# Post-norm chains on the vector engine by pairs of k-tiles, and 1/rms of memory attention in the exponential

## The chip, the cores and the metric

One core of one Trainium2 chip runs the whole program. The metric is the device time of one execution in microseconds (us). Engines: TensorE (PE, with its weight loads as PEld), the vector engine (DVE), the scalar engine (ACT), GpSimd (POOL), and the queue that issues most DMAs (SP). Each runs its own instruction queue in order; they wait for one another through semaphores.

## The reference

Two transformer blocks in float32 on 512 tokens of width 1024. The change lies in the second block, between its mixer and its feed-forward layer:

```python
def rms_norm(x, g):
    y = x * lax.rsqrt(jnp.mean(x * x, axis=-1, keepdims=True) + RMS_EPS)
    return y * g

# second_block
x = x + rms_norm(merged @ w_mix_out, mix_post_g)
h = rms_norm(x, xa_pre_g)
x = x + rms_norm(mem_attention(h, mem_n, w_xq, w_xkv, w_xo), xa_post_g)
h = rms_norm(x, ffn_pre_g)
x = x + rms_norm(conv_ffn(h, w_up, conv_w, conv_b, w_down), ffn_post_g)

# mem_attention: 4 heads of 128, 256 memory tokens
q = h @ w_xq;  s = q @ k.T / sqrt(128);  p = softmax(s);  o = p @ v;  return o @ w_xo
```

## The kernel before

Activations lie with features on the 128 partitions and the 512 tokens along the free axis, so a tensor of width 1024 is 8 k-tiles of 128 x 512. `X` is the running sum x. Every matmul in float32 precision is three matmuls in a reduced form (lines L195 to L197, in `mm3`): operands are split into a rounded part (`qhi`, `whi`) and its residue (`qlo`, `wlo`). Weights are loaded tile by tile and split by `wsplit`: the cast on the scalar engine (L186), the subtraction (L187) on the vector engine, or on GpSimd if the caller says so (`lo_eng`).

The work around the change runs over two halves of the tokens, 256 columns each (`HALVES`). `fm` computes output tiles m one after the other, and between the matmuls it takes steps of a generator (`between`), which holds the chain of the half before. The order in which the queues hold the work comes from a scheduler that follows the program's order and priorities, not from a table.

The stages, with their tiles: the merge projection (`w_mix_out`, 8 tiles, the last 5 in halves); the query projection of memory attention (`w_xq`, 4 tiles, one for each head) and its output projection (`w_xo`, 8 tiles of 4 k-tiles), both for the first half and then for the second; the first three pairs of tiles of the up projection (`w_up`), in halves, then the others over 512 columns.

`post` makes what stands between two projections. `ev` evicts a tile times its gain into `Y` (`Ym` or `KV`), and adds its square to `sqs`. `after` is the chain of a half: 1/rms of the tile (`r_post`, by sums over partitions in TensorE and `rms`), its broadcast over partitions (`bcast`, L330, copied to `rbp`), and then for each of the 8 k-tiles Y times `rbp` (L1404), X plus Y (L1405), the split of X times the next gain into `qhi` and `qlo` (`pre`, L1357 and L1358), and the square of X (L1411), of which GpSimd adds up two groups of four (L1415). These are summed by TensorE (`sums`, L312) into `r_pre`, the 1/rms of the next norm, which is broadcast into `rb`. The next projection runs on X times gain, and its result is multiplied by `rb` when it leaves the accumulator: L1643 for the query (`xq`), L1723 for the up projection (`z`).

`head_half` is one head for one half: `xq`; for each 128 tokens the scores (L1647), their maximum (L1652), the exponential with its sum (L1654), reciprocal and normalisation; then transposes (L1668), the product with v (L1673), and the split of the result into `xh` (L1674, L1675), which the output projection reads. `pair2` evicts a pair of tiles of the up projection, applies the convolution and the Gelu (L1733).

Of the kernel before, what the change touches and what calls it, by code (L numbers as in the profile page):

```python
# [10 lines left out]
F32 = mybir.dt.float32  # L11
# [9 lines left out]
S = 512  # L21
# [38 lines left out]
LQ, LO = 0, 1  # L60
# [20 lines left out]
def kernel(ctx: ExitStack, tc: tile.TileContext, a: dict, out: bass.AP, stop=None):  # L81
# [43 lines left out]
    def col(name, i):  # L125
        o = COLS[name][0] + i
        return cols[:, o:o + 1]
# [1054 lines left out]
    X = []  # L1182

    def load_x():
        for i, tag in enumerate(("og", "cg")):
            t = xs.tile([128, 4, S], F32, tag=tag, name=f"X{i}")
            nc.sync.dma_start(t, a["xT"][:, 4 * i:4 * i + 4])
            X.extend(t[:, k] for k in range(4))

# [73 lines left out]
    def add_sq(src, m, x, y, eng=V):  # L1263
        if m == 0:
            A.activation(sqs[:, x:y], src, AF.Square)
        else:
            t = sp.tile([128, S], F32, tag="sqt", name="sqt")
            A.activation(t[:, x:y], src, AF.Square)
            eng.tensor_tensor(sqs[:, x:y], sqs[:, x:y], t[:, x:y], ALU.add)
# [115 lines left out]
    def post(Y, gname, nextg, g2):  # L1385

        def ev(m, x, y, p):
            if YA and y - x < S:
                A.activation(Y(m, x, y), p, AF.Copy, scale=col(gname, m))
            else:  # L1390
                V.tensor_scalar(Y(m, x, y), p, col(gname, m), None, ALU.mult)
            add_sq(p, m, x, y, G if AQ and y - x < S else V)

        def after(x, y):
            rbp = sp.tile([128, S // 2], F32, tag="rbp", name="rbp")
            r = fm_stats(sp, sqs[:, x:y], "post")
            yield
            bcast(rbp, r)
            pt = sums()
            for k in range(KT + PL):  # L1400
                if k > 1:
                    yield
                if k < KT:
                    V.tensor_tensor(Y(k, x, y), Y(k, x, y), rbp, ALU.mult)  # L1404
                    (V if k in XV else G).tensor_tensor(X[k][:, x:y], X[k][:, x:y], Y(k, x, y), ALU.add)  # L1405
                j = k - PL
                if j >= 0:
                    pre(g2, nextg, j, x, y)
                    first, end = j in SQS, j + 1 in SQS
                    t = sp.tile([128, S // 2], F32, tag="n2t" if first else "sqx", name="sqx")  # L1410
                    A.activation(t, X[j][:, x:y], AF.Square)  # L1411
                    if first:
                        held = t
                    else:
                        G.tensor_tensor(held, held, t, ALU.add)  # L1415
                    if end and j < KT - 1:
                        tc.cur_priority += SL
                        sum_sq(pt, held, j + 1 == SQS[1], False)
                        tc.cur_priority -= SL
            yield  # L1420
            sum_sq(pt, held, len(SQS) == 1, True)
            r = rms(sp, pt, (y - x) // 128, "pre")
            yield
            bcast(rb[:, x:y], r)
        return ev, after

# [195 lines left out]

    xa = ExitStack()
# [6 lines left out]
    ev, after = post(lambda k, x, y: Ym[:, k, x:y], "mix_post_g", "xa_pre_g", g4)  # L1630
# [9 lines left out]
    def head_half(h, x, y, p):  # L1640

        xq = xt.tile([128, S // 2], F32, tag="xq", name="xq")
        V.tensor_tensor(xq, p, rb[:, x:y], ALU.mult)  # L1643
        soft = []
        for t in range((y - x) // 128):
# [5 lines left out]
            sc = 128 ** -0.5  # L1651
            V.tensor_reduce(mx, s_[:, :MEM], AX, ALU.max)  # L1652
            V.tensor_scalar(mx, mx, -sc, None, ALU.mult)
# [36 lines left out]
    ev, after = post(lambda k, x, y: KV[:, k] if x else Ym[:, k, x:y], "xa_post_g", "ffn_pre_g", g4)  # L1690
# [20 lines left out]
    with tc.tile_pool(name="fp2", bufs=1) as fp:  # L1711
        zl = fp.tile([128, 2, 4, 2], F32, name="zl")

        def pair2(pg_, pu_, i, x, y, held):
            res = []
# [189 lines left out]
```

## Time and profile before

| | |
|---|---|
| Timed runs (3) | 1681.08, 1681.2, 1683.91 us; median 1681.2 |
| Profiled execution | 1677.47 us, span of its instructions 1675.7 us |
| Mean granted clock of TensorE | 0.984 |
| Busy: TensorE, vector, scalar, GpSimd | 96%, 57%, 43%, 19% |

A busy share is an average over all stages. What a stage can gain is read from the windows and waits of that stage. A time in the timeline is counted from the start of the span; the matmuls' ends are modelled, so that the distance of two starts says more than a duration. "Granted clock" is the share of TensorE's full rate of 2.4 GHz; half of it is 1.2 GHz.

### The profile page before, as it was taken

To read this page: it belongs to the slowest core of one execution; us is meant where nothing else is said; L and a number is where in the kernel's file an instruction comes from. 1 tells how busy PE (TensorE), PEld (TensorE's weight loads), DVE (VectorE), ACT (ScalarE), POOL (GpSimd) and SP (SyncE) were. 2 spreads that over 40 slices of the span, in tenths; PEclk is the share of its full clock that TensorE was granted. 3 is DMA by queue.
4 is the path that set the end of the run, shared out by engine and by line. 5 is a ranking of instruction groups with operands and counts; after the bars stand their busy time and mean duration, and the time that the engine had idled before them with its cause. 6 is when DMAs were issued, how large, how long until landed. Compare 5 with 4: busy or idle time off the path is not lost.

```text
span 1675.7 us, 25585 instructions
## 1 busy us (share of the span) xinstructions
PE 1605.1 (96%) x10116; PEld 1362.9 (81%) x10116; DVE 954.5 (57%) x1728; ACT 721.6 (43%) x1374; POOL 325.5 (19%) x354
## 2 busy tenths in 40 slices
PE   9999989989999999999999999999888999999997
PEld 6898777668899888888888777888887888888886
DVE  6547887777666222223335776345677877776233
ACT  4525455566645322232223664234455544444221
POOL 1313310231111222210004000132423222221002
PEclk9999999989999999999999999999899899999998
DMA  9222244231323333333332212335110233233332
GB/s 377 60 80 65 95 142 156 68 122 64 126 76 102 91 98 99 91 97 102 88 115 85 63 39 64 101 95 181 42 35 26 76 101 97 92 101 94 95 92 73
DMA packets 47465, 161.95 MB, mean 97 GB/s; under 512 B 5488, under 2 KB 10096, under 8 KB 45552
## 3 DMA queue, kind: packets, MB, share of 16 engines
q1 hardware_dynamic: 44752, 157.74, 29.7%
q10 hardware_dynamic: 2304, 2.29, 0.4%
q8 instruction: 80, 1.31, 0.3%
q0 software_dynamic: 288, 0.28, 0.1%
q14 instruction: 41, 0.34, 0.1%
HBM read 157.41 MB, written 3.15 MB: 96 GB/s over the span
## 4 chain that ended last, share of the span: by engine, by line
PE 81%; DVE 10%; ACT 3%; DMA 2%; issue 2%; POOL 1%; ACTq 0%; SPq 0%; DVEq 0%; POOLq 0%
PE acc L196 15%; PE acc L195 15%; PE acc L197 15%; PE s L195 5%; PE s L196 5%; PE s L197 5%; PE acc L285 2%; PE acc L284 2%; PE acc L286 2%; DVE wlo L187 1%; PE mis L1094 1%; PE mis L1573 1%; DVE Ym L1404 1%; DVE qlo L1358 1%; ACT whi L186 1%
## 5 line engine op out<-in xcount | busy, mean ns | idle before, releaser
L186 ACT CAST whi<-wf 128x1024 fp32r<-128x1024 f32 (+4 forms) x221 | 228.4, 1035 | 427.1 <-PE acc L196 289.8
L187 DVE TENSOR_TENSOR wlo<-wf,whi 128x1024 fp32r<-128x1024 f32 (+2 forms) x183 | 224.2, 1225 | 178.3 <-ACT whi L186 173.0
L195 PE MATMUL acc<-qhi,whi 128*128 128x512 f32 (+1 forms) x640 | 240.4, 376 | 0.0
L197 PE MATMUL acc<-qhi,wlo 128*128 128x512 f32 (+1 forms) x640 | 240.1, 375 | 0.0
L196 PE MATMUL acc<-qlo,whi 128*128 128x512 f32 (+1 forms) x640 | 240.0, 375 | 0.0
L197 PEld LDWEIGHTS acc<-qhi,wlo 128*128 128x128 f32 x640 | 122.1, 191 | 19.5
L196 PEld LDWEIGHTS acc<-qlo,whi 128*128 128x128 f32 x640 | 121.7, 190 | 19.8 <-issue 0.2
L195 PEld LDWEIGHTS acc<-qhi,whi 128*128 128x128 f32 x640 | 121.9, 190 | 19.5
L187 POOL TENSOR_TENSOR wlo<-wf,whi 128x1024 fp32r<-128x1024 f32 x38 | 91.0, 2395 | 209.8 <-ACT whi L186 209.8
L196 PE MATMUL s<-qlo,whi 128*128 128x512 f32 (+1 forms) x336 | 127.6, 380 | 0.0
L195 PE MATMUL s<-qhi,whi 128*128 128x512 f32 (+1 forms) x336 | 127.5, 379 | 0.0
L197 PE MATMUL s<-qhi,wlo 128*128 128x512 f32 (+1 forms) x336 | 127.3, 379 | 0.0
L1368 DVE TENSOR_TENSOR e<-e,s 128x512 f32<-128x512 f32 (+1 forms) x22 | 14.3, 652 | 154.0 <-PE s L197 153.8
L196 PE MATMUL acc<-glo,whi 128*128 128x512 f32 (+1 forms) x208 | 74.3, 357 | 0.1
L195 PE MATMUL acc<-ghi,whi 128*128 128x512 f32 (+1 forms) x208 | 74.4, 358 | 0.0
L197 PE MATMUL acc<-ghi,wlo 128*128 128x512 f32 (+1 forms) x208 | 74.2, 357 | 0.0
L195 PEld LDWEIGHTS s<-qhi,whi 128*128 128x128 f32 x336 | 63.2, 188 | 11.9
L197 PEld LDWEIGHTS s<-qhi,wlo 128*128 128x128 f32 x336 | 63.1, 188 | 11.9
L196 PEld LDWEIGHTS s<-qlo,whi 128*128 128x128 f32 x336 | 63.2, 188 | 11.7
L195 PE MATMUL acc<-Fhi,whi 128*128 128x512 f32 (+1 forms) x187 | 71.6, 383 | 0.0
L196 PE MATMUL acc<-Flo,whi 128*128 128x512 f32 (+1 forms) x187 | 71.5, 383 | 0.0
L197 PE MATMUL acc<-Fhi,wlo 128*128 128x512 f32 (+1 forms) x187 | 71.5, 382 | 0.0
(648 smaller groups left out, 3951.3 us busy)
## 6 DMA issues: line engine op xcount, KB each, us to landing
wf<-in_w_ffn_in SPq DMA_DIRECT2D x44, 512.0 KB, 3.5
wf<-in_w_up SPq DMA_DIRECT2D x44, 512.0 KB, 3.5
wm<-in_w_mod SPq DMA_DIRECT2D x32, 512.0 KB, 4.1
wm<-in_w_mod SPq DMA_DIRECT2D x8, 1024.0 KB, 13.6
wf<-in_w_ffn_out SPq DMA_DIRECT2D x16, 512.0 KB, 3.5
wf<-in_w_g SPq DMA_DIRECT2D x16, 512.0 KB, 3.6
wf<-in_w_down SPq DMA_DIRECT2D x16, 512.0 KB, 3.6
X<-in_xT SPq DMA_DIRECT2D x4, 1024.0 KB, 5.5
```

The costliest lines, as they stand in the source:

```text
L186: A.copy(hi[:, :n], wf[:, :n])
L187: (lo_eng or V).tensor_tensor(lo[:, :n], wf[:, :n], f32(hi[:, :n]), ALU.subtract)
L195: T.matmul(o, lhi, rhi, start=start, stop=False)
L196: T.matmul(o, lhi, rlo, start=False, stop=False)
L197: ins = T.matmul(o, llo, rhi, start=False, stop=stop).ins
L284: T.matmul(o, bhi(k), whi, start=k == 0, stop=False)
L285: T.matmul(o, bhi(k), wlo, start=False, stop=False)
L286: T.matmul(o, blo(k), whi, start=False, stop=k == KT - 1)
L1094: T.matmul(p[:, :128], aT[:, kt * 128:(kt + 1) * 128], v, start=kt == 0, stop=kt == NKT - 1)
L1358: V.scalar_tensor_tensor(g2[1][:, k, x:y], X[k][:, x:y], col(gname, k), f32(g2[0][:, k, x:y]), ALU.mult, ALU.subtract)
L1404: V.tensor_tensor(Y(k, x, y), Y(k, x, y), rbp, ALU.mult)
L1573: T.matmul(pO[:, ts], vz[:, kt, hp_, 64 * e:64 * e + 128], pT[:, kt * 128:(kt + 1) * 128], start=kt + e == 0, stop=kt - t + e == 1, skip_g ...
```

## The change

In `post`, both for the merge projection and for memory attention:

- Evictions of halves go from the scalar to the vector engine.
- The chain takes two k-tiles at a time: one multiply of 2 x 256 columns with `rbp` repeated, one addition to X over the pair, and one square over the pair on the scalar engine. All additions are on the vector engine, GpSimd has none left. All four squares of pairs are added into one tile `held` (`hld`), 2 x 256 columns.
- The sums over partitions, 1/rms and its broadcast are no longer part of the chain. They become a function `tail`, put into a table by half, and `ready` calls it where the value is first needed: for memory attention in the first `head_half` of a half, for the up projection in the first `pair2` of a half.

In `head_half` the query is copied without `rb` (on the scalar engine); 1/rms of a token, times 128 ** -0.5, becomes `rsc`, one column for each 128 tokens, which scales the maximum and is the scale operand of the exponential. So for memory attention 1/rms is not broadcast any more. `LO` goes from 1 to 0: the residues of `w_xo` are subtracted on the vector engine, not on GpSimd.

```diff
-LQ, LO = 0, 1
+LQ, LO = 0, 0
...
-    def post(Y, gname, nextg, g2):
+    def post(Y, gname, nextg, g2, tails, spread):
 
         def ev(m, x, y, p):
-            if YA and y - x < S:
-                A.activation(Y(m, x, y), p, AF.Copy, scale=col(gname, m))
-            else:
-                V.tensor_scalar(Y(m, x, y), p, col(gname, m), None, ALU.mult)
-            add_sq(p, m, x, y, G if AQ and y - x < S else V)
+            V.tensor_scalar(Y(m // 2 * 2, x, y)[:, m % 2], p, col(gname, m), None, ALU.mult)
+            add_sq(p, m, x, y)
 
         def after(x, y):
             rbp = sp.tile([128, S // 2], F32, tag="rbp", name="rbp")
             r = fm_stats(sp, sqs[:, x:y], "post")
             yield
             bcast(rbp, r)
-            pt = sums()
-            for k in range(KT + PL):
-                if k > 1:
...
+            yield
+            rb2 = rbp.rearrange("p (o t) -> p o t", o=1).to_broadcast([128, 2, S // 2])
+            held = hq.tile([128, 2, S // 2], F32, tag="hld", name="hld")
+            for k in range(0, KT + 2, 2):
+                if k < KT:
+                    y2, x2 = Y(k, x, y), XT[k // 4][:, k % 4:k % 4 + 2, x:y]
+                    V.tensor_tensor(y2, y2, rb2, ALU.mult)
+                    V.tensor_tensor(x2, x2, y2, ALU.add)
+                    for j in (k, k + 1):
+                        A.activation(g2[0][:, j, x:y], X[j][:, x:y], AF.Copy, scale=col(nextg, j))
+                    t = held if k == 0 else sp.tile([128, 2, S // 2], F32, tag="sqx", name="sqx", bufs=1)
+                    A.activation(t, x2, AF.Square)
+                    yield
+                if k > 0:
+                    for j in (k - 2, k - 1):
+                        V.scalar_tensor_tensor(g2[1][:, j, x:y], X[j][:, x:y], col(nextg, j), f32(g2[0][:, j, x:y]),
+                                               ALU.mult, ALU.subtract)
+                    if k > 2:
+                        V.tensor_tensor(held, held, last, ALU.add)
                     yield
                 if k < KT:
...
+                    last = t
+
+            def tail():
+                pt = sums()
+                for j in range(2):
+                    sum_sq(pt, held[:, j], j == 0, j == 1)
+                r = rms(sp, pt, (y - x) // 128, "pre")
+                if spread:
+                    bcast(rb[:, x:y], r)
+                return r
+            tails[x] = tail
         return ev, after
+
+    def ready(tails, x):
+
+        if callable(tails.get(x)):
+            tails[x] = tails[x]()
+        return tails.get(x)
...
-        V.tensor_tensor(xq, p, rb[:, x:y], ALU.mult)
+        A.copy(xq, p)
+        if x not in rsc:
+            rsc[x] = xt.tile([128, 2], F32, tag="rsc", name="rsc")
+            V.tensor_scalar(rsc[x], ready(rq_of, x), 128 ** -0.5, None, ALU.mult)
...
-            sc = 128 ** -0.5
+            sc = rsc[x][:, t:t + 1]
             V.tensor_reduce(mx, s_[:, :MEM], AX, ALU.max)
-            V.tensor_scalar(mx, mx, -sc, None, ALU.mult)
+            V.scalar_tensor_tensor(mx, mx, -1.0, sc, ALU.mult, ALU.mult)
             A.activation(sm, s_[:, :MEM], AF.Exp, bias=mx, scale=sc, accum_out=l)
...
         def pair2(pg_, pu_, i, x, y, held):
+            ready(rb_of, x)
             res = []
```

TensorE's queue, where the query projection of the first half ends its first tile (`acc<-qhi,whi` and its like are query matmuls, `s_...<-KV,xq` the scores of the first head, `mis<-ones,sqs` the sums for the other half's `r_post`). Before:

```order
L330 MATMUL mis<-ident,r_pre 128x128 x2
L312 MATMUL mis<-ones,sqs 128x32 x2
L197 MATMUL acc<-qhi,wlo 128x256
L195 MATMUL acc<-qhi,whi 128x256
L196 MATMUL acc<-qlo,whi 128x256
L197 MATMUL acc<-qhi,wlo 128x256
L195 MATMUL acc<-qhi,whi 128x256
L196 MATMUL acc<-qlo,whi 128x256
L197 MATMUL acc<-qhi,wlo 128x256
L1647 MATMUL s_11405<-KV,xq 128x256
L1647 MATMUL s_11415<-KV,xq 128x256
```

After:

```order
L195 MATMUL acc<-qhi,whi 128x256
L312 MATMUL sums<-ones,hld 128x32 x4
L1663 MATMUL s_11387<-KV,xq 128x256
L1663 MATMUL s_11397<-KV,xq 128x256
L312 MATMUL mis<-ones,sqs 128x32 x2
L196 MATMUL acc<-qlo,whi 128x256
L197 MATMUL acc<-qhi,wlo 128x256
L195 MATMUL acc<-qhi,whi 128x256
L196 MATMUL acc<-qlo,whi 128x256
L197 MATMUL acc<-qhi,wlo 128x256
L195 MATMUL acc<-qhi,whi 128x256
```

The broadcast of `r_pre` is gone; the sums (`sums<-ones,hld`), in before 26 rows further up, and the scores stand behind the first tile with only one matmul of the next before them.

The vector engine's queue at the same place, from the 1/rms of the first half on (`t_pre`, `r_pre`: its steps; `mx`: maxima of the scores; `kl`, `xw`, `wlo`: residues of weights). Before:

```order
L163 TENSOR_SCALAR v_pre<-sums 128x2
L187 TENSOR_TENSOR wlo<-wf,whi 128x1024
L1269 TENSOR_TENSOR sqs<-sqs,sqt 128x256
L166 TENSOR_TENSOR t_pre<-y_pre 128x2
L167 TENSOR_TENSOR t_pre<-t_pre,v_pre 128x2
L168 TENSOR_SCALAR t_pre<-t_pre 128x2
L169 TENSOR_TENSOR r_pre<-y_pre,t_pre 128x2
L163 TENSOR_SCALAR v_post<-mis 128x2
L1643 TENSOR_TENSOR xq<-acc,rb 128x256
L1652 TENSOR_REDUCE mx<-s_11405 128x1
L166 TENSOR_TENSOR t_post<-y_post 128x2
```

After, from a little further on:

```order
L187 TENSOR_TENSOR wlo<-wf,whi 128x1024
L168 TENSOR_SCALAR t_pre<-t_pre 128x2
L166 TENSOR_TENSOR t_post<-y_post 128x2
L187 TENSOR_TENSOR kl<-kf,kh 128x1024
L169 TENSOR_TENSOR r_pre<-y_pre,t_pre 128x2
L167 TENSOR_TENSOR t_post<-t_post,v_post 128x2
L187 TENSOR_TENSOR kl<-kf,kh 128x1024
L1659 TENSOR_SCALAR rsc<-r_pre 128x2
L168 TENSOR_SCALAR t_post<-t_post 128x2
L187 TENSOR_TENSOR xw<-wf,xw 128x1024
L1669 SCALAR_TENSOR_TENSOR mx<-mx,rsc 128x1 x2
L169 TENSOR_TENSOR r_post<-y_post,t_post 128x2
```

The multiply `xq` is gone, and four splits that GpSimd had, two `kl` and two `xw`, stand between the steps of 1/rms and the scaled maximum. The exponential of the first head takes this maximum.

The scalar engine's queue in the up projection, where the 1/rms of the second half stands (`y_pre`), after the change (`early`: the first half's pairs; L1750 is the Gelu):

```order
L1750 ACTIVATE early<-early 128x256
L186 CAST whi<-wf 128x1024
L1341 CAST ghi<-early 128x256
L186 CAST whi<-wf 128x1024
L164 ACT_TABLE_LOAD
L164 ACTIVATE y_pre<-v_pre 128x2
L165 ACT_TABLE_LOAD
L165 ACTIVATE y_pre<-y_pre 128x2
L186 CAST whi<-wf 128x1024
L331 COPY rb<-mis 128x256
L1744 ACTIVATE zc_12672<-z,cols 128x256
L1744 ACTIVATE zc_12679<-z,cols 128x256
```

Before, the two `y_pre` rows stood ahead of the first Gelu and of the only table load of this part; now two loads go with them, and one more follows for the next Gelu.

## Rows read from the trace of the kernel before

**Rows 1.** The page, busy time of each engine, share of the span, instructions

```profile
PE 1605.1 (96%) x10116; PEld 1362.9 (81%) x10116; DVE 954.5 (57%) x1728; ACT 721.6 (43%) x1374; POOL 325.5 (19%) x354
```

**Rows 2.** Windows: length, busy us of PE, PEld, DVE, ACT, POOL; clock, DMA, GB/s

```profile
1195.50:1237.90 42.40, 32.18 (x198) 29.19 (x198) 35.74 (x83) 24.36 (x65) 21.94 (x20) 0.88 0.15 51
1237.90:1247.10 9.20, 9.20 (x77) 8.99 (x77) 2.53 (x7) 5.40 (x15) 0.00 (x0) 1.00 0.00 0
1247.10:1277.30 30.20, 26.76 (x191) 24.34 (x191) 25.66 (x73) 18.86 (x54) 9.46 (x12) 1.00 0.16 48
...
1286.50:1309.00 22.50, 15.86 (x106) 15.00 (x105) 18.46 (x33) 11.32 (x26) 11.34 (x19) 0.77 0.07 24
```

**Rows 3.** Waits of PE in 1195.5 to 1237.9: total, times, longest

```profile
PE s L1647 <- DVE xq L1643: 3.9, 3, 1.8
PE mis L330 <- DVE r_pre L169: 3.4, 1, 3.4
PE sums L312 <- POOL sqx L1415: 2.4, 1, 2.4
```

**Rows 4.** Timeline of PE: start, us, engine, line, operation

```profile
1200.37 0.41 PE L195 MATMUL acc<-qhi,whi 128*128 128x256 f32 x1
1200.58 0.41 PE L196 MATMUL acc<-qlo,whi 128*128 128x256 f32 x1
...
1203.44 0.28 PE L197 MATMUL acc<-qhi,wlo 128*128 128x256 f32 x1
1203.56 0.28 PE L195 MATMUL acc<-qhi,whi 128*128 128x256 f32 x1
```

**Rows 5.** Timeline of DVE, 1189 to 1234

```profile
1189.78 0.41 DVE L1404 TENSOR_TENSOR Ym<-Ym,rbp 128x256 f32<-128x256 f32 x1
1190.11 0.47 DVE L1358 SCALAR_TENSOR_TENSOR qlo<-X,cols,qhi 128x256 fp32r<-128x256 f32 x1
...
1192.27 0.97 DVE L1404 TENSOR_TENSOR Ym<-Ym,rbp 128x256 f32<-128x256 f32 x1
...
1202.19 2.34 DVE L166 TENSOR_TENSOR t_pre<-y_pre 128x2 f32<-128x2 f32 x1
...
1233.64 0.34 DVE L1659 TENSOR_SCALAR sm<-sm,l 128x256 f32<-128x256 f32 x1
```

**Rows 6.** Timeline of POOL, same time

```profile
1192.02 0.92 POOL L1405 TENSOR_TENSOR X<-X,Ym 128x256 f32<-128x256 f32 x1
...
1202.06 4.76 POOL L187 TENSOR_TENSOR kl<-kf,kh 128x1024 fp32r<-128x1024 f32 x2 [3.47 <-ACT kh L186]
```

**Rows 7.** Groups of DVE by form: count, busy us, mean ns, idle before

```profile
L187 DVE TENSOR_TENSOR wlo<-wf,whi 128x1024 fp32r<-128x1024 f32 x158 | 196.4, 1243 | 150.8 <-ACT whi L186 145.6 <-PE acc L197 1.6
...
L1269 DVE TENSOR_TENSOR sqs<-sqs,sqt 128x512 f32<-128x512 f32 x17 | 11.7, 686 | 0.1
...
L661 DVE TENSOR_TENSOR kdv<-kdv,r_qk 128x1536 f32<-128x1536 f32 x2 | 3.5, 1750 | 0.1
```

**Rows 8.** Groups of DVE, 1195.5 to 1237.9

```profile
L1652 DVE TENSOR_REDUCE mx<-s 128x1 f32<-128x256 f32 x8 | 3.2, 415 | 2.4 <-PE s L1647 2.3
...
L1655 DVE RECIPROCAL l<-l 128x1 f32<-128x1 f32 x8 | 1.2, 154 | 0.1
```

**Rows 9.** Waits of PE in 1286.5 to 1333

```profile
PE sums L312 <- POOL sqx L1415: 3.4, 1, 3.4
```

**Rows 10.** Timeline of DVE, first tiles of the up projection

```profile
1291.36 2.53 DVE L1404 TENSOR_TENSOR KV<-KV,rbp 128x256 f32<-128x256 f32 x4 [1.27 <-ACT rbp L331]
...
1303.30 1.21 DVE L187 TENSOR_TENSOR Flo<-wf,Fhi 128x1024 fp32r<-128x1024 f32 x1
```

**Rows 11.** Timeline of ACT, around the table load

```profile
1313.65 0.20 ACT L165 ACTIVATE y_pre<-y_pre 128x2 f32<-128x2 f32 x1
1313.87 1.28 ACT L1733 ACT_TABLE_LOAD   x1
1315.16 0.72 ACT L1733 ACTIVATE early<-early 128x256 f32<-128x256 f32 x2
```

More of the change, by code (lines that the diff above doesn't have):

```diff
@@ L1180, in diff_merge @@
         V.scalar_tensor_tensor(mlo[:, 4 + h], p, gd, f32(mhi[:, 4 + h]), ALU.mult, ALU.subtract)
-    X = []
+    X, XT = [], []
     def load_x():
@@ L1187, in load_x @@
             nc.sync.dma_start(t, a["xT"][:, 4 * i:4 * i + 4])
+            XT.append(t)
             X.extend(t[:, k] for k in range(4))
@@ L1402, in after @@
                     yield
                 if k < KT:
[L1404 to L1424, printed above, removed]
+                    last = t
[7 more added lines that the diff above has]
+                return r
@@ L1620 @@
     m2.close()
+    hq = ctx.enter_context(tc.tile_pool(name="hq", bufs=1))
     xa = ExitStack()
@@ L1629 @@
     Ym = xp.tile([128, KT, S], F32, name="Ym")
-    ev, after = post(lambda k, x, y: Ym[:, k, x:y], "mix_post_g", "xa_pre_g", g4)
+    rq_of, rb_of, rsc = {}, {}, {}
+    ev, after = post(lambda k, x, y: Ym[:, k:k + 2, x:y], "mix_post_g", "xa_pre_g", g4, rq_of, False)
     for ms, segs in tail_halves(T1):
@@ L1689, in head_step @@
             heads.pop(i)
-    ev, after = post(lambda k, x, y: KV[:, k] if x else Ym[:, k, x:y], "xa_post_g", "ffn_pre_g", g4)
+    ev, after = post(lambda k, x, y: KV[:, k:k + 2] if x else Ym[:, k:k + 2, x:y], "xa_post_g", "ffn_pre_g", g4, rb_of, True)
     xk = kept(xp, (-3, -2, -1, 2), NF)
```

## The prediction

> **What bounds the kernel now.** Read the page first: TensorE is busy 96% of the span [rows 1]; over most of the program nothing on another engine can move the end. The change touches about 180 us of it, from the merge projection to the first tiles of the up projection, so I cut that part with the windows view [rows 2]. In the two stretches of memory attention, and in the first tiles of the up projection, TensorE falls to 32.2 of 42.4, 26.8 of 30.2 and 15.9 of 22.5 us, twice at a mean granted clock below 1 (0.88, 0.77), while the vector engine is busy 84, 85 and 82% of the time. The 9.2 us between the two attention stretches (output projection of memory attention) are full of matmuls at clock 1.00. So the three stretches, not the tiles between them, can shrink.
>
> The waits of TensorE in the first stretch name the places [rows 3]: 3.9 us for `xq`, which is the query tile times 1/rms; 3.4 us for the 1/rms itself (`r_pre`); 2.4 us for the sum of squares that GpSimd adds. After such a wait the next matmuls start 0.21 us apart, later ones of the same shape 0.12 us [rows 4]: half rate, 1.2 against 2.4 GHz.
>
> The timelines of DVE and POOL show why the vector engine is slow here. A 256-column multiply takes 0.41 us, and the next operation starts 0.33 us after it; beside a GpSimd add of 0.92 us the same multiply takes 0.97 [rows 5, 6]. A two-column multiply takes 2.34 us beside GpSimd's two weight splits [rows 5, 6]. The two engines work in turns here. The change takes all of GpSimd's work out of these chains.
>
> **The change part by part.** I count the vector engine's own time in a stretch, since its queue is in order and the end of a stretch is its last `xh` write. Each operation overlaps the next by about 0.07 us (0.41 against 0.33 [rows 5]), so I take durations less 0.07.
>
> The pair operation on two k-tiles (512 elements, one operand repeated over the pair) does not stand in the trace in that shape. Below it is bounded by the plain 512-column form, 0.69, above by two contended 256-column ones, 2 x 0.97 = 1.94 [rows 5, 7]. A form with 6 x 256 elements and a repeated operand takes 1.75 for 1536 elements [rows 7], 1.04 ns for each element above the 512 of the plain one, so the repeat costs nothing: I take 0.69, own time 0.62. The eviction of 256 columns moves from the scalar to the vector engine; not seen there, it lies between the small 0.15 and the 512-column 0.69 [rows 7, 8]; I take the 256-column 0.41.
>
> First attention stretch (42.4 us). Vector work after the change: pair operations 12 x 0.62 = 7.4 (9 of the second half's chain, 3 left over from the first); residues `qlo` 9 x 0.40 = 3.6 (0.47 in the quiet [rows 5]); 3 leftover evictions and sums x 0.34 = 1.0; weight splits, now 6 instead of 2, since four leave GpSimd, 6 x 1.17 = 7.0 [rows 7]; four heads with 8 maxima x 0.35, 8 normalisations x 0.27, 4 `xh` x 0.34, and 16 column operations x 0.1, together 8.0 [rows 5, 8]; two rms chains 1.7. Sum 28.7 against 35.7 busy before [rows 2]: 7.0 us less, although the engine does more. With the idle 6.7 us of before (42.4 - 35.7) the stretch is 7.0 shorter. Walking the new order row by row, I find less idle: the query tiles no longer stop for `r_pre`, so all four are multiplied without a break, and the second half's chain starts some 6 us earlier. But TensorE then waits about 6 us in pieces at the end, behind the heads. I take -8. Bounds: idle shrinks to 2 us (-12), or grows by 4 us, because the first exponentials are queued behind two casts of the output weights on the scalar engine, and the `rsc` they need behind four splits (-3).
>
> Second attention stretch (30.2 us): 11 pair operations 6.8, 8 `qlo` 3.2, 2 splits 2.3, heads 8.0, rms 1.7, together 22.0 against 25.7. That is -3.7 with the same idle; the last two `xh` writes are now queued behind the chain's last addition, which waits for a square on the scalar engine, so I take -2.5 (bounds -5 and +1.5).
>
> Front of the up projection (22.5 us). TensorE waits 3.4 us for GpSimd's sums [rows 9] and then for the split of the next weights, whose vector half starts at 1303.30 [rows 10]. In the new order there stand before it, from 1291.36 on, 8 pair operations (5.0), 6 `qlo` (2.4), 1 sum (0.6), 4 column operations of the other half's rms (0.6) and 2 evictions (0.7): 9.3, so it starts at 1300.7, 2.6 us earlier. I take -2.6 (bounds -4 and -1).
>
> What the change adds: the second half's 1/rms is now emitted at its first use, after the Gelu table is loaded. The scalar queue then holds, behind the first half's Gelus, a weight cast, a table load, the logarithm, a second load, the exponential, and later a third load for the next Gelu, where before there was one load. One load takes 1.28 us [rows 11]. From the end of the tile that triggers it: cast 1.05 (an estimate, under the 1.24 of the vector half of the same split [rows 7]), load 1.28, 0.2, load 1.28, 0.2, four column operations 0.8, some 0.3 between engines: 5.1 us. TensorE's broadcast stands 26 matmuls and the sums later in its queue, 26 x 0.12 + 0.5 = 3.6 us of cover. What is late is 1.5 us: +1.5 (bounds +0.5 and +3). Behind the broadcast are queued the rest of that tile and two more; the vector engine's evictions wait for it too.
>
> About these loads the Trainium skill speaks against the change: "ScalarE: Activation LUTs", section "What ACT_TABLE_LOAD costs", gives about 1283 ns for the load and another 1380 ns of drain for each switch. Here the load agrees, but the exponential before it began 0.22 us earlier and ended 0.02 before it, and the Gelu starts 0.01 after it [rows 11], so no drain shows.
>
> Costed at nothing: the evictions on the vector engine inside the output projection (0.75 us of vector work a tile where TensorE needs 12 x 0.12 = 1.4; if that cover goes, three accumulators still stand between); the copy of the query on the scalar engine, whose removed evictions pay for it; the two broadcasts that fall away; the merge projection itself, where TensorE does not wait.
>
> Sum: -8 - 2.5 - 2.6 + 1.5 = -11.6. The profiled execution took 1677.5 us (span 1675.7 and 1.8 around it), so 1665.9 for such a one. The median of the timed runs is 3.7 us higher, 1681.2; I put the forecast on that: 1669.6 us.
>
> **The rivals.**
> (a) Half rate at the sparse ends. The heads now run behind the query tiles, so TensorE goes into the output projection after a thin passage of small matmuls and waits. If it then runs at 1.2 GHz for the following 78 output and 24 query matmuls of both halves, that is 204 x 0.092 = 18.8 us: 1688.4, slower. It decides from 126 such matmuls on (11.6 / 0.092), and is slower beyond noise from 163. For it speak the half-rate matmuls after the waits of before [rows 3, 4]; against it that the 9.2 us after an equally thin end had clock 1.00 [rows 2].
> (b) Only the front gains. The heads are held not by vector work but by the round trips between four engines; then just the stops for the sum and for `r_pre` go (2.4 and 3.4, with no saved clock), and the last two terms: -5.8 - 2.6 + 1.5 = -6.9 if all of it stays, and with half of the 5.8 given back to the later heads -4.0: 1677.2. For it: TensorE's longest total wait is in the heads. Against: the vector engine's 84%.
> (c) The change frees the vector engine, and the time turns into its idle time: 7.0 + 3.7 + 2.6 us of busy time saved, no place earlier, because casts in the scalar queue set the pace. 1681.
> (d) Each table switch also drains, 1.38 us by no row here, twice before the 1/rms: 1669.6 + 2.8 = 1672.4. The rows around the one load speak against it. This is the rule of the Trainium skill's page on ScalarE named above.
>
> **How the numbers follow.** Forecast 62%, own range 1663.5 to 1676 (its terms' bounds: -20.5 and +0.3 if all go one way, about half of that to be expected). (a) 9%, (b) 14%, (c) 9%, (d) 6%. I call 0.2%, 3.4 us, the limit of what a measurement of this kernel can tell from no change: faster than 1677.8. Faster: nearly all of the forecast (0.60), most of (b) (0.11), (d) 0.06: 0.77. Same: the rest of the forecast and (b), most of (c): 0.13. Slower: (a) and a little of (c): 0.10. The range 1663 to 1679.5 leaves out (a), most of (c) and the ends of the forecast.
>
> **What would show it.** Right: vector multiplies on pairs at 0.69 us; none of TensorE's waits for `r_pre` and the sums between the first two query tiles; stretch ends (the last `xh` of each half) some 8 and then 10 us earlier; the second weight split of the up projection about 13 us earlier; one wait of 1 to 2 us at the last `r_pre` broadcast, with three more table loads. Wrong: pair operations well over 0.7; a granted clock below 1 in the output projection; exponentials of the first head later than before; the last broadcast waiting more than 3 us.

## The result, and the profile after

| | before | after |
|---|---|---|
| Median of the first timed runs | 1681.14 us (4 runs) | 1659.91 us (4 runs) |
| Ratio, 95% interval | | 0.9872 [0.9857, 0.9888] |
| Again in another job | 1676.76 us (9 runs) | 1661.50 us (5 runs), 0.9911 [0.9898, 0.9925] |
| Profiled execution, its span | 1677.47, 1675.7 us | 1659.84, 1656.3 us |

Faster by the prediction's own limit of 0.2%, as forecast, but by 15 to 21 us instead of 11.6, and outside the range of 1663 to 1679.5. The engines' busy times [rows 1] after:

```profile
PE 1600.3 (97%) x10108; PEld 1358.7 (82%) x10108; DVE 948.8 (57%) x1756; ACT 715.9 (43%) x1341; POOL 278.5 (17%) x302
```

The windows that answer to [rows 2]: first attention stretch, output projection, second stretch, output projection, front of the up projection, its second part (columns as there). As in [rows 2] and in the prediction, a stretch ends with its last `xh` write.

```profile
1192.85:1223.33 30.48, 28.03 (x187) 25.38 (x186) 27.30 (x77) 20.05 (x55) 0.00 (x0) 0.94 0.22 70
1223.33:1232.70 9.37, 8.85 (x75) 8.65 (x73) 7.20 (x18) 3.33 (x8) 0.00 (x0) 1.00 0.01 2
1232.70:1259.63 26.93, 26.93 (x199) 25.15 (x198) 22.43 (x72) 19.22 (x53) 0.00 (x0) 1.00 0.13 40
1259.63:1268.91 9.28, 9.28 (x79) 9.28 (x78) 6.61 (x15) 2.69 (x7) 0.00 (x0) 1.00 0.16 57
1268.90:1288.70 19.80, 14.44 (x101) 13.55 (x100) 16.38 (x40) 12.87 (x26) 2.36 (x7) 0.83 0.12 32
1288.70:1313.75 25.05, 24.20 (x207) 24.00 (x205) 17.83 (x42) 15.07 (x26) 6.14 (x11) 1.00 0.32 102
```

The writes that end them, the first half before, then both halves after:

```profile
1237.48 0.42 DVE L1675 TENSOR_TENSOR xh<-mis,xh 128x256 fp32r<-128x256 f32 x1 [0.44 <-ACT xh L1674]
```

```profile
1222.91 0.42 DVE L1691 TENSOR_TENSOR xh<-mis,xh 128x256 fp32r<-128x256 f32 x1 [0.50 <-ACT xh L1690]
1258.84 0.79 DVE L1691 TENSOR_TENSOR xh<-mis,xh 128x256 fp32r<-128x256 f32 x2
```

The first stretch fell from 42.4 to 30.48 us and the second from 30.1 to 26.93. The output projections behind them kept their length: 9.3 us up to the next stage's first matmul before, 9.4 and 9.3 after. TensorE's waits in the first stretch and the output projection [rows 3], and its first query matmuls [rows 4]:

```profile
PE mis L1684 <- ACT qhi L1407: 1.9, 1, 1.9
PE acc L195 <- ACT sqs L1266: 0.5, 1, 0.5
PE mis L1684 <- ACT xpT L1685: 0.5, 1, 0.5
```

```profile
1192.85 0.28 PE L195 MATMUL acc<-qhi,whi 128*128 128x256 f32 x1
1192.96 0.28 PE L196 MATMUL acc<-qlo,whi 128*128 128x256 f32 x1
1193.09 0.28 PE L197 MATMUL acc<-qhi,wlo 128*128 128x256 f32 x1
```

The waits for the sums, for 1/rms and for `xq` are gone, and the first matmuls start 0.12 us apart. In the up projection the wait for GpSimd's sums [rows 9] is gone, and one for a cast stands there. Waits from 1268.9 to 1313.8:

```profile
PE s L195 <- ACT Fhi L186: 4.9, 1, 4.9
PE mis L330 <- DVE r_pre L169: 0.8, 1, 0.8
PE s L197 <- DVE Flo L187: 0.5, 1, 0.5
```

**One ruler for all runs.** In the timeline of TensorE I take five starts: the merge projection's first sums over partitions; the first query matmul of the second half; the first matmul of the up projection; its first tile of 512 columns; the last broadcast of the program. The first four, of before and then of after:

```profile
1181.16 0.41 PE L312 MATMUL mis<-ones,sqs 128*128 128x32 f32 x2
1247.17 0.27 PE L195 MATMUL acc<-qhi,whi 128*128 128x256 f32 x1
1286.54 0.27 PE L195 MATMUL acc<-qhi,whi 128*128 128x256 f32 x1
1332.60 0.40 PE L195 MATMUL acc<-qhi,whi 128*128 128x512 f32 x1
```

```profile
1178.77 0.30 PE L312 MATMUL mis<-ones,sqs 128*128 128x32 f32 x1
1232.70 0.28 PE L195 MATMUL acc<-qhi,whi 128*128 128x256 f32 x1
1268.91 0.28 PE L195 MATMUL acc<-qhi,whi 128*128 128x256 f32 x1
1313.75 0.40 PE L195 MATMUL acc<-qhi,whi 128*128 128x512 f32 x1
```

Their differences are S1 (end of the merge projection, first attention half), S2 (second half) and S3 (first tiles of the up projection). From there to the last broadcast it took 334.14 to 334.16 us in every run. Time is the run's median, in brackets the ratio to before of the same job with its interval; without brackets it is one execution (for before the median of four).

| Run | S1 | S2 | S3 | sum, us | time, us |
|---|---|---|---|---|---|
| before | 66.01 | 39.37 | 46.06 | 151.44 | 1681.14 |
| before_again | 65.99 | 39.40 | 46.20 | 151.59 | 1676.28 |
| after | 53.93 | 36.21 | 44.84 | 134.98 | 1659.91 (0.9872) |
| after_again | 52.51 | 36.21 | 46.01 | 134.73 | 1661.50 (0.9911) |
| g_off | 51.88 | 35.53 | 43.68 | 131.09 | 1658.15 (0.9881 [0.9863, 0.9899]) |
| lo0_only | 59.09 | 39.41 | 46.21 | 144.71 | 1672.31 |
| adds_only | 58.20 | 35.51 | 44.12 | 137.83 | 1661.72 |
| exp_only | 64.02 | 40.04 | 46.17 | 150.23 | 1676.68 (0.9994 [0.9984, 1.0004]) |
| g_off_exp | 51.39 | 35.29 | 43.85 | 130.53 | 1656.30 (0.9869 [0.9851, 0.9887]) |
| g_back | 62.46 | 39.75 | 46.74 | 148.95 | 1674.85 (0.9986 [0.9977, 0.9996]) |
| lo1 | 61.69 | 34.82 | 45.09 | 141.60 | 1668.97 (0.9951 [0.9938, 0.9963]) |
| q_rb | 52.47 | 37.03 | 45.51 | 135.01 | 1661.33 (0.9906 [0.9892, 0.9919]) |
| eager_up | 52.50 | 37.42 | 44.34 | 134.26 | 1659.34 (0.9898 [0.9884, 0.9911]) |
| after_ya | 51.30 | 35.71 | 45.09 | 132.10 | 1659.81 |
| pairs | 53.57 | 35.45 | 43.18 | 132.20 | 1659.60 |
| fill | 72.43 | 39.38 | 46.52 | 158.33 | 1683.06 |
| fill_order | 68.82 | 39.38 | 46.43 | 154.63 | 1679.49 |
| slots | 52.51 | 36.21 | 38.25 | 126.97 | 1652.74 (0.9858 [0.9844, 0.9871]) |
| best_b | 51.31 | 35.27 | 40.64 | 127.22 | 1652.00 (0.9856 [0.9842, 0.9869]) |
| best_c | 51.65 | 35.30 | 38.23 | 125.18 | 1650.29 (0.9837 [0.9824, 0.9851]) |

Of unchanged kernels the sum repeats within 0.25 us, single stages within 1.5, while whole executions of before lie between 1674.3 and 1683.9. So the parts are compared by the sum.

### The profile page after: what moved, and what is told of

It is laid out like the page before. It is cut to its first block, busy times and chain, and to the rows that moved or that the text cites. A ratio compares the mean times of both kernels' runs of the same rounds, so it can differ in the third digit from the quotient of the medians.

```text
span 1656.3 us, 25493 instructions
## 1 busy us (share of the span) xinstructions
PE 1600.3 (97%) x10108; PEld 1358.7 (82%) x10108; DVE 948.8 (57%) x1756; ACT 715.9 (43%) x1341; POOL 278.5 (17%) x302
## 4 chain that ended last, share of the span: by engine, by line
PE 85%; DVE 7%; ACT 4%; DMA 2%; issue 1%; POOL 1%; ACTq 0%; SPq 0%; DVEq 0%; POOLq 0%
PE acc L195 16%; PE acc L196 16%; PE acc L197 16%; PE s L195 5%; PE s L196 5%; PE s L197 5%; PE acc L284 2%; PE acc L285 2%; PE acc L286 2%; PE mis L1094 1%; PE mis L1584 1%; DVE wlo L187 1%; PE acc L721 1%; PE mis L1086 1%; PE s L1065 1%
## 5 line engine op out<-in xcount | busy, mean ns | idle before, releaser
L197 PEld LDWEIGHTS s<-qhi,wlo 128*128 128x128 f32 x336 | 63.2, 188 | 11.9
L195 PEld LDWEIGHTS s<-qhi,whi 128*128 128x128 f32 x336 | 63.2, 188 | 11.9
```

What stands on the lines that cost most here:

```text
L195: T.matmul(o, lhi, rhi, start=start, stop=False)
L197: ins = T.matmul(o, llo, rhi, start=False, stop=stop).ins
```

## The experiments

Theory 1: the chain of the vector engine and GpSimd, which work in turns, sets the length of S1. Theory 2: the stop of the query tiles for 1/rms does, with the half rate behind it.

**The two kernels again.** No edit.

> The kernel before, unchanged, profiled a second time. The after kernel reached the merge projection's first sums over partitions 2.4 us earlier than the before kernel (1178.77 against 1181.16 us), ahead of every changed instruction. If that is a difference between executions, this profile puts them somewhere between 1177 and 1183 and other waits ahead of 510 us come and go; if it belongs to the before kernel (its layout in memory), they stand at 1181.2 within 0.3 again, with the same waits. Time 1678 to 1684.

> The changed kernel, unchanged, again beside the kernel before. From the merge projection's first sums over partitions (L312) to the first tile of 512 columns of the up projection it took 134.98 us, the kernel before 151.44 and 151.59 in two profiles; what lies outside that stretch differed by up to 2.6 us between executions of kernels that have the same instructions there. So: 135.0 within 0.3 for the stretch, and a difference of 16.5 to 19 us in the medians.

The first sums stood at 1179.90 in before_again and at 1181.76 in after_again, the reverse of the first pair: what lies ahead of the chain is a difference between executions. The change is worth 151.5 - 134.9 = 16.7 us (means of two). The medians of that job differ by 15.3, less than the 16.5 to 19 expected.

**One part alone, on the kernel before.**

```diff
 g_off:
-XV = (3, 7)
+XV = range(8)
-LQ, LO = 0, 1
+LQ, LO = 0, 0
-                        G.tensor_tensor(held, held, t, ALU.add)
+                        V.tensor_tensor(held, held, t, ALU.add)
 exp_only:
-        V.tensor_tensor(xq, p, rb[:, x:y], ALU.mult)
+        A.copy(xq, p)
+        if x not in rsc:
+            rsc[x] = xt.tile([128, 2], F32, tag="rsc", name="rsc")
+            V.tensor_scalar(rsc[x], rq_of[x], 128 ** -0.5, None, ALU.mult)
...
+            sc = rsc[x][:, t:t + 1]
```

g_off_exp has both; lo0_only has the second edit of g_off, adds_only the first and third.

> The kernel before with GpSimd emptied in these chains: all additions to X and of squares, and the residues of w_xo, on the vector engine; single k-tiles, 1/rms of the query and its broadcast as before. Theory 1 (turns between GpSimd and the vector engine are the main cost): the first attention stretch shrinks by 6 or more of 42.4 us although the vector engine does more, vector multiplies at 0.41 us, time about 1670. Theory 2 (the stop of the query tiles for 1/rms and the half rate after it are the main cost): the wait for r_pre stays at 2 us or more, query matmuls stay 0.2 us apart, the stretch loses 3 or less, time about 1677.

> The kernel before with one part of the change: the query is copied on the scalar engine, 1/rms of memory attention goes into the exponential's scale and is not broadcast; chains and GpSimd as before. Theory 1: only the 3.4 us wait for r_pre goes and half of it comes back in the heads, time about 1679. Theory 2: the query tiles run on without a stop, most of their matmuls at 0.12 us, the first attention stretch is 6 to 9 us shorter, time about 1673.

> Both parts on the kernel before: GpSimd emptied, and 1/rms of memory attention in the exponential; no pairs, no late sums, evictions of halves on the scalar engine. If the two parts add up: 12 to 14 us under before, 1667 to 1669, and pairs and late sums bring the last 7 to 9 us. If pairs hardly matter (theory 2 says that the vector engine is no bound once TensorE does not stop): 1661 to 1664. If single operations on one engine are too many (theory 1's other side: 12 more per half on the vector engine): 1672 or more.

> The kernel before with one flag changed: the residues of w_xo on the vector engine instead of GpSimd; the chain's additions stay on GpSimd. On the changed kernel the reverse edit (lo1) cost 6.6 us of the touched stretch, all in the first half. If the two parts add up: 145 us for the touched stretch instead of 151.5. If the additions still hold the chain up: 149 to 151.

> The kernel before with the chain's additions all on the vector engine (12 more operations of 0.42 us for each half of a chain) and the residues of w_xo still on GpSimd. On the changed kernel the reverse edit (g_back) cost 14.1 us. If the two parts add up: 137 to 138 us for the touched stretch. If the weight splits on GpSimd alone still hold the vector engine in the first half as long as in lo1: 139 to 141.

Theory 2 falls. exp_only has no stop for 1/rms left; it gained 1.3 us of the sum and nothing measurable in time: TensorE just waited later, among the heads. adds_only, with the weight splits still on GpSimd, keeps the stop and gained 13.7 us all the same:

```profile
PE mis L330 <- DVE r_pre L169: 3.9, 1, 3.9
```

g_off, in which the query still waits for the broadcast of 1/rms, gained 20.4, more than the whole change and more than theory 1 expected. Its list of TensorE's waits has no row for `r_pre`: the stop went with GpSimd's work. The windows of its S1 in two pieces (cut at the first query matmul), after those of before:

```profile
1181.16:1199.11 17.95, 15.44 (x127) 14.93 (x125) 15.63 (x27) 12.10 (x30) 10.40 (x12) 1.00 0.08 30
1199.11:1247.17 48.06, 40.34 (x266) 37.26 (x266) 34.69 (x84) 26.38 (x74) 19.34 (x16) 0.89 0.13 45
```

```profile
1179.86:1194.42 14.56, 14.55 (x123) 14.35 (x121) 12.23 (x36) 11.28 (x29) 0.00 (x0) 1.00 0.11 37
1194.42:1231.74 37.32, 36.30 (x270) 33.92 (x270) 32.54 (x104) 26.05 (x75) 0.00 (x0) 1.00 0.19 58
```

The vector engine runs 140 instructions there instead of 111 (36 + 104, 27 + 84), and yet its busy time falls by 5.5 us (50.3 to 44.8): this is contended time that went. Its idle time falls by 8.6 (15.7 to 7.1), which I had not seen. The cut at the last `xh` tells where:

```profile
1194.42:1221.73 27.31, 26.32 (x191) 24.35 (x191) 25.21 (x82) 18.95 (x54) 0.00 (x0) 1.00 0.26 78
1221.73:1231.74 10.01, 9.98 (x82) 9.58 (x81) 7.34 (x23) 7.10 (x21) 0.00 (x0) 1.00 0.01 2
```

In the stretch the idle time fell from 6.7 to 2.1 us. The rest of the fall lies in the output projection, where the vector engine had little to do before (2.5 us [rows 2]) and now does 7.3 us of work that is left over from the chain. In the stretch of before, 4.1 us of its idle time stood directly behind the late 1/rms, while TensorE made the sums and the first scores:

```profile
1209.30 0.16 DVE L163 TENSOR_SCALAR v_post<-mis 128x2 f32<-128x2 f32 x1 [2.07 <-PE mis L312]
1211.81 0.42 DVE L1652 TENSOR_REDUCE mx<-s 128x1 f32<-128x256 f32 x1 [2.01 <-PE s L1647]
```

The two parts of g_off give 6.8 and 13.7 us alone and 20.4 together: they add up. Not separated is how much of the 13.7 is vector operations held up beside an addition, and how much is the addition itself, 0.92 us in the chain on GpSimd [rows 6] and 0.42 on the vector engine.

**One part undone, on the changed kernel.**

```diff
 g_back:
-                    V.tensor_tensor(x2, x2, y2, ALU.add)
+                    (V if k == 6 else G).tensor_tensor(x2, x2, y2, ALU.add)
-                        V.tensor_tensor(held, held, last, ALU.add)
+                        G.tensor_tensor(held, held, last, ALU.add)
 lo1:
-LQ, LO = 0, 0
+LQ, LO = 0, 1
 q_rb:
-        A.copy(xq, p)
...
+        ready(rq_of, x)
+        V.tensor_tensor(xq, p, rb[:, x:y], ALU.mult)
...
 eager_up:
-            tails[x] = tail
+            tails[x] = tail() if spread else tail
```

> The changed kernel with GpSimd back in the chains: it adds three of four pairs to X and all pairs of squares. Theory 1: vector multiplies beside it take twice as long, 6 to 9 us slower than the changed kernel, about 1667. Theory 2: 2 to 3 us slower, about 1662, since the query tiles still do not stop.

> The changed kernel with the residues of the output projection's weights on GpSimd again, as before. Theory 1: each of its four splits of some 2.4 us holds up the vector engine's chain and heads beside it, 2 to 4 us slower, about 1663. Theory 2: within 1 us of the changed kernel, since 4.7 us of vector work leave the stretch at the same time.

> The changed kernel with one part undone: 1/rms of memory attention is broadcast again and multiplied into the query on the vector engine; pairs, one engine and sums at first use stay. Theory 1 (turns between the engines): 1 to 3 us slower than the changed kernel, about 1662. Theory 2 (the stop for 1/rms and the half rate after it): TensorE waits 2 us or more for r_pre ahead of the first scores, 5 to 8 us slower, about 1666.

> The changed kernel with the sums, 1/rms and broadcast of the up projection emitted at the end of their chain again, not at first use; memory attention's stay late. My term for the late emission was +1.5 us, so without it the three extra table loads and the wait at the last broadcast go: 1658.4. The other side: the sums stand ahead of the next tile in TensorE's queue again and it waits there for the last addition of squares, 1 to 3 us more: 1661 to 1663.

GpSimd's additions cost 14.1 us and its weight splits 6.7, each about twice what theory 1 expected; undoing the exponential costs nothing (135.0 against 134.9). eager_up gained 0.6 of the sum: my +1.5 for the late emission has the right sign, less than half the size. lo1 shows the turns best. DVE in one piece, beside a weight split on POOL:

```profile
1212.03 0.15 DVE L1669 SCALAR_TENSOR_TENSOR mx<-mx,rsc 128x1 f32<-128x1 f32 x1
1212.20 2.38 POOL L187 TENSOR_TENSOR xw<-wf,xw 128x1024 fp32r<-128x1024 f32 x1 [13.32 <-ACT xw L186]
1212.26 0.42 DVE L1668 TENSOR_REDUCE mx<-s 128x1 f32<-128x256 f32 x1
1212.72 1.88 DVE L1669 SCALAR_TENSOR_TENSOR mx<-mx,rsc 128x1 f32<-128x1 f32 x1
1214.63 0.56 ACT L1670 ACTIVATE sm<-s,mx,rsc 128x256 f32<-128x256 f32 x1 [1.41 <-DVE mx L1669]
```

One operation on one column, 0.15 us by itself, takes 1.88: it ends 0.02 us after GpSimd's instruction (1214.60 and 1214.58), and the exponential waits for it. The maximum between them, which reads the scores that TensorE wrote, keeps its 0.42. The Trainium skill ("SBUF — State Buffer", section "SBUF: two separate sides") says that the vector engine and GpSimd share one pair of ports as an exclusive lock, that whichever starts first holds it for its whole instruction, and that a vector operation with two inputs from SBUF needs it; these rows agree.

**Evictions, and pairs.** after_ya is the changed kernel with the halves evicted by `A.activation(..., AF.Copy, scale=col(gname, m))` again; pairs undoes the exponential and the late sums besides.

> The changed kernel with the evictions of halves on the scalar engine again. If the evictions (some 0.34 us of vector work each, 16 in the two output projections) are what the changed kernel loses against g_off: 131 to 133 us for the touched stretch instead of 134.9. If the late sums and the pairs are: 134.5 to 135.5.

> The changed kernel with all but the pairs and the single engine undone: the query times 1/rms on the vector engine, sums and broadcast at the chain's end, evictions of halves on the scalar engine. Beside g_off (131.1 us for the touched stretch, single k-tiles) it shows the pairs alone. If pairs save vector work that bounds (0.69 for two against 2 x 0.41): 128 to 130. If they lengthen the way from one k-tile to the next engine, since the scalar engine gets two k-tiles only after both are done: 133 to 135, as the changed kernel.

The evictions on the vector engine cost 2.8 us (134.9 to 132.1). Pairs cost 1.1 against single k-tiles (132.2 and 131.1). The sum of the parts: -20.4 GpSimd, +2.8 evictions, +1.1 pairs, -0.6 exponential (g_off_exp against g_off), +0.6 late sums, together -16.5 of the measured -16.7.

**Is it the clock?** Both kernels keep TensorE busy with matmuls that nothing reads, in the waits of before, for the first half only. The edit of fill_order:

```diff
...
+            fill(20)
             sum_sq(pt, held, len(SQS) == 1, True)
...
+            tc.cur_priority += late
+            fill(26)
             bcast(rb[:, x:y], r)
+            tc.cur_priority -= late
```

> The kernel before with 46 extra matmuls of 256 columns into an unused tile, 20 in front of the sum that waited for GpSimd (2.4 us) and 26 in front of the broadcast of 1/rms that waited 3.4 us; nothing reads them. Theory 1 (the vector engine and GpSimd set the length): the granted clock of the first attention stretch rises from 0.89, query matmuls run 0.12 us apart, and its end stays where it was: 47 to 49 us from the first query tile to that of the second half (48.06 before). Theory 2 (the half rate costs time itself): 4 to 5 us shorter, 43 to 44.

> The kernel before with 46 extra matmuls of 256 columns into an unused tile that nothing reads: 20 ahead of the sum that waited 2.4 us for GpSimd, 26 between the last matmuls of the first query tile and the broadcast of 1/rms that waited 3.4 us. Theory 1 (the chain on the vector engine and GpSimd sets the length): query matmuls run at 0.12 us, and from the merge projection's first sums to the second half's first query tile it takes 65 to 67 us (66.0 before). Theory 2 (the half rate costs time itself): 61 to 62.

fill has no change of priority and 28 extra matmuls in the second place, and so came out with the broadcast of 1/rms ahead of the first query tile. It tells of that order alone: a stop of 8.8 us, S1 6.4 longer. In fill_order the first query tile ran 0.12 us a matmul from its second one on, and TensorE then waited longer:

```profile
1198.32 0.36 PE L195 MATMUL acc<-qhi,whi 128*128 128x256 f32 x1
1198.52 0.28 PE L196 MATMUL acc<-qlo,whi 128*128 128x256 f32 x1
...
1210.84 0.77 PE L330 MATMUL mis<-ident,r_pre 128*128 128x128 f32 x2 [5.80 <-DVE r_pre L169]
```

S1 was 2.8 us longer, not 4 to 5 shorter. It is no clean zero, since the vector engine's order moved too: the broadcast of 1/rms came 30.5 us after the first sums, 26.2 before. So a faster TensorE alone gave nothing in this run; how much of the 12 to 13.5 us is clock stays open. The two profiles of the changed kernel give a hint of the size. The second took 1.0 us less in the first stretch, at a granted clock of 1.00 instead of 0.94, with the vector engine as busy as in the first; whether the clock made this difference is not shown:

```profile
1195.84:1225.31 29.47, 26.99 (x190) 24.54 (x189) 27.18 (x77) 19.94 (x55) 0.00 (x0) 1.00 0.23 72
```

**The new wait.** Why does the cast `Fhi` come so late? The scalar engine was idle ahead of it:

```profile
1281.44 0.68 DVE L1405 TENSOR_TENSOR X<-X,KV 128x512 f32<-128x512 f32 x1
```

```profile
1282.15 1.05 ACT L186 CAST Fhi<-wf 128x1024 fp32r<-128x1024 f32 x1 [0.97 <-DVE X L1405]
```

It reads nothing from the vector engine, but starts 0.03 us after the last addition that reads `KV`. `Fhi` lies in a pool that takes over the memory of `KV` and `Ym`. The kernel before has the same wait, behind the one for the sums:

```profile
1301.51 0.41 DVE L1405 TENSOR_TENSOR X<-X,KV 128x256 f32<-128x256 f32 x1
1301.95 1.05 ACT L186 CAST Fhi<-wf 128x1024 fp32r<-128x1024 f32 x1 [0.98 <-DVE X L1405]
1303.10 0.55 PE L195 MATMUL s<-qhi,Fhi 128*128 128x256 f32 x1 [2.42 <-POOL zl L1725]
```

The profile puts these 2.42 us down to GpSimd, but the matmul reads `Fhi`, and starts 0.10 us after the cast. So TensorE's two waits here, 3.4 and 2.4 us, became one of 4.9. slots puts two weight tiles into `ghi` and `glo`, whose memory was last read by the output projection:

```diff
...
-        room = [None] * 3 + [(room[j], room[5 + j], None) for j in range(5)]
+        room = [(room[j], room[5 + j], None) for j in range(5)]
+        room = [None] * 3 + [tuple(sl[:, k:k + 2].rearrange("p k s -> p (k s)") for sl in slot) + (None,) for k in spare] + room
...
```

> The changed kernel with one edit that the change doesn't have: the fourth and fifth split weight tile of the up projection go into memory whose last reader is the output projection, not into memory that holds the tiles KV and Ym until the chain's last addition. Theory 1 (the 4.9 us wait for the cast Fhi is a wait for memory: the cast starts 0.03 us after the addition that last reads KV): the cast moves up by 10 us, the wait goes, 3 to 5 us faster than the changed kernel. Theory 2 (the vector engine bounds the front: two evictions and the split's subtraction stand behind the chain): the wait only moves to the next tile, within 1 us.

> A candidate for a kernel faster than both: the kernel before with GpSimd emptied and 1/rms in the exponential (g_off_exp, 130.5 us for the touched stretch), the weight tiles in other memory as in slots, and both sums of the last chain at its end. Theory 1: TensorE's waits of 3.0 us for the sums and 1.5 us for the cast in the front of the up projection go, with the half rate behind them: 4 to 5 us less, 126 us for the stretch, about 1652. Theory 2: the vector engine bounds the front, 129 to 131.

> GpSimd emptied with single k-tiles, 1/rms in the exponential, weight tiles in other memory as in slots, and the last chain's sums, 1/rms and broadcast at the first use as in the changed kernel. In best_b the front of the up projection took 40.64 us with a wait of 2.0 us at the last broadcast, in slots 38.25 with 0.8. If the parts add up (36.7 + 35.3 + 14.6 + 38.3): 124.9 us for the touched stretch, 2 us under slots, about 1650.5. If the shorter stretches only move the same work of the vector engine into the front: 126.5 to 127.5.

Here spare is (6, 4), two pairs of k-tiles that are written later. In slots the cast begins 13 us earlier in the timeline, the wait is gone, and the sum fell by 7.9 us, more than the 3 to 5 expected and all of it in S3: the stop and the half rate behind it (clock 0.83 above). The cast in slots:

```profile
1269.17 1.05 ACT L186 CAST ghi<-wf 128x1024 fp32r<-128x1024 f32 x1 [0.47 <-PE acc L197]
```

best_c puts together what paid: GpSimd emptied, single k-tiles, evictions on the scalar engine, 1/rms in the exponential, slots, and the last chain's sums at first use. The parts add up (125.2; 124.9 expected). It is faster than both kernels: 0.9837 [0.9824, 0.9851] of before, where the changed kernel has 0.9872 and 0.9911. Its clock in S3 is 1.00:

```profile
1269.02:1307.25 38.23, 36.46 (x304) 35.99 (x302) 30.84 (x79) 26.45 (x50) 9.20 (x17) 1.00 0.22 71
```

## Why the prediction was wrong in size

- **The step that failed: the size of the first attention stretch, -8.** It gave 11.9 us (42.4 to 30.48; 12.9 in the second profile), at its bound of -12 and beyond it. My -8 was the vector engine's own time, 28.7 us by count, and, by what is left of 34.4, 5.7 us of idle time, as if the engine were held by its load and its idle time hardly moved. Measured are 27.3 and 3.2 us (27.2 and 2.3 in the second profile): the count was 1.4 us high, the idle time 2.5 to 3.4. What stood in its place is shown by g_off: with nothing on GpSimd the contended time and the idle time both go, and its stretch of 27.31 us has 2.1 idle, although 1/rms is still broadcast there. That the 9.2 us of output projection behind the stretch would stay was right: 71 of its 96 matmuls were left after the last `xh`, before and after (68 in the second profile).
- **The removed stop for 1/rms** stood in my reasons for that -8. It was no cause: adds_only keeps it and gains 13.7 us, and exp_only removes it and gains 1.3. The 1/rms was late because its short vector operations each waited out a weight split on GpSimd (2.34 us [rows 5], where such a one takes 0.15 alone), and in g_off the stop is gone without the exponential.
- **Pair operations** took 0.68 us, as predicted (0.69), but start 0.60 us apart where two single ones take 0.67: 0.07 us to gain on each, and 1.1 us lost in all.
- **Evictions on the vector engine**, costed at nothing since TensorE's 1.4 us a tile would hide them: 2.8 us.
- **Second stretch** -2.5: measured -3.2 (30.1 to 26.93). **Front of the up projection** -2.6: measured -2.7 (22.5 to 19.8). The count of vector work ahead of the split of [rows 10] was right: 9.34 us from the chain's first multiply, 9.3 predicted, 11.94 before. The split began 20 us earlier and not 13, since the first stretch gave more and the whole chain began 2.4 us earlier in this execution. What the prediction did not see is that TensorE stood there for memory, as it had before.

```profile
1273.89 0.69 DVE L1404 TENSOR_TENSOR KV<-KV,rbp 128x512 f32<-128x512 f32 x1 [1.21 <-ACT rbp L331]
1283.23 1.22 DVE L187 TENSOR_TENSOR Flo<-wf,Fhi 128x1024 fp32r<-128x1024 f32 x1
```

- **Late sums** +1.5: the next stage grew by 1.45 (23.60 to 25.05), with a wait of 0.8 us at the broadcast; in the sum of all stages they cost 0.6.
- **The base.** I put the sum on 1681.2, the median of three runs. In later jobs before had medians of 1676.8 to 1677.8 (9 to 17 runs). On such a base -11.6 gives 1665 to 1666, and the measured -16.7 gives 1660 to 1661, where the kernel is. So of the 9.7 us that the forecast was high about 5 are the terms (4 to 5 of them the first stretch), the rest the base. Why the first runs of before were 4 us slower than the later ones no run shows; on the later base the range would have lain 4 us lower, with the measured time just inside its edge. (The bounds of the terms add up to -20.5 and +0.5, not +0.3.)

The rivals: (a) no half rate in the output projection, clock 1.00 there; (b) allowed 6.9 us at most, and the first stretch alone gave 11.9. (c) The freed time did not turn into idle time of the vector engine: in the first stretch its busy time fell by 8.4 us and its idle time by 3.5. (d) the table loads, [rows 11] after:

```profile
1301.18 1.28 ACT L164 ACT_TABLE_LOAD   x1
1302.47 0.20 ACT L164 ACTIVATE y_pre<-v_pre 128x2 f32<-128x2 f32 x1
1302.69 1.28 ACT L165 ACT_TABLE_LOAD   x1
1303.99 0.20 ACT L165 ACTIVATE y_pre<-y_pre 128x2 f32<-128x2 f32 x1
```

Each switch is 1.28 us, with 0.01 to 0.02 us on either side. The drain of 1380 ns that the Trainium skill names ("ScalarE: Activation LUTs", section "What ACT_TABLE_LOAD costs") does not show in these rows.

## What to carry to other kernels

Where the vector engine and GpSimd work on one chain, price a GpSimd instruction by the vector operations that stand still beside it and by the round trips through them, not by busy time: here 14 us for additions that the vector engine takes on at 0.42 us each. A stretch is as long as an engine's own time only if that engine is never idle in it; ask of the idle part what ends it. And when a cast or a load waits for an engine whose result it doesn't read, look for the memory that it takes over.

## What the runs showed of the hardware

- A vector operation on one or two columns took 1.9 to 2.3 us beside a GpSimd instruction of 2.4 (0.15 alone). In the kernel before the operation after the one of 2.34 us in [rows 5] lost a turn too, so that these two alone made 1/rms more than 4 us late:

```profile
1204.57 2.26 DVE L167 TENSOR_TENSOR t_pre<-t_pre,v_pre 128x2 f32<-128x2 f32 x1
```

- Executions of the kernel before differ by up to 9.6 us (1674.3 to 1683.91), while the touched 135 to 151 us repeat within 0.25 and the 334 us after them are the same within 0.02 in all runs.
